# DeltaNet scan: the q-k matrices stored as full 128x128 blocks, one product a step, and buffers regrouped

## The chip, the cores and the metric

The kernel runs on one core of one Trainium2 chip. The core has a matrix engine (TensorE, PE in the rows, with PEld for the loading of its stationary operand), a vector engine (VectorE, DVE), a scalar engine (ScalarE, ACT), GpSimd (POOL), and SyncE (SP), which issues most DMAs. Each engine runs its own list of instructions in order, and waits for the others by semaphores. The metric is the device time of one execution in microseconds; less is better. All numbers are from the profiler's record of one execution, or from timed runs where this is said.

## The reference

One encoder layer over 768 tokens (a prompt of 256 and a sample of 512) with 1024 columns: a modulated norm, one input projection, eight heads of windowed attention beside four heads of a gated DeltaNet that runs forward and backward, an output projection, a second modulated norm and a gated feed-forward part. The change is in the DeltaNet. Its tokens are cut into chunks of 64, and each head and direction goes through its chunks with a state `S`:

```
a_mat = lower + jnp.eye(CHUNK)                      # lower = strict(kb k^T * decay)
u = triangular_solve(a_mat, v * beta)
w = triangular_solve(a_mat, kb * exp(gc))
intra = where(causal, (q k^T) * decay, 0)           # the q-k matrix of a chunk

def step(S, xs):
    v_new = u_i - w_i S
    o = q_i S + intra_i v_new
    S = S * exp(gl_i) + k_i^T v_new
```

## The kernel before

The program is written as ordinary code; a scheduler lays its instructions out for each engine by priority, and a pool hands out buffers by tag: a new tile under a tag with `bufs=1` can be written only when the last reader of the tile before it under that tag is done. So a tag that two tiles share is a wait, and a change of tags can change the order on every engine.

The heads of the DeltaNet are worked off in two pairs, called 0 and 1 here. For each pair:

- `dn_proj` makes q, k and v with the projection products L476. [...] The same line, with `z_proj`, and later `att_proj` (L868) serve as filler: they depend on little, and the scheduler puts them between the products of the scans and the solves.
- `dn_decay` (L616 to L629) makes the decay matrices: products L620, four `affine_select` on POOL, one exponential on ACT (L629).
- `dn_gram` (L634 to L651) multiplies them with k k^T and q k^T. The products L642 and L643 use 64 columns of the array each. The q-k matrices go into `Ic`, with 64 columns for each chunk.
- `dn_solve` inverts the triangular matrices. DVE does blocks of 16 by substitution (L691 and L693, 15 rounds, after the transpose L680 and the two L687, and before the transposes L695 and L700 and the two L701 and L702); PE joins them in levels (L708, L729). The result is `Wbd`.
- `dn_scan` (L752 to L806) goes through 24 steps: prompt and sample, two heads each, of four and eight steps. A step works on a forward and a backward chunk at once. On PE it has two products L768 (`S` against k and q), one L782 (`Wbd` times `r`), two L793 (the state's update) and two L802 (`Ic` times the new values). Between them DVE makes `r` (L774), half of `XS` (L786), the new `S` (L796) and the output (L806); ACT makes `tm` (L781), the other half of `XS` (L788) and the two copies `XB` (L790) of 64x128 each.

The two products of L802 take 64 columns of `Ic` each and write the two halves of the rows of one PSUM block `ps4`. Each takes a copy `XB` whose other half of rows is zero, which POOL has cleared once (L462), so that the forward chunk doesn't mix with the backward one:

```
for e in range(2):                                           # L789
    nc.scalar.copy(xb[half(e), e, :], ps2[half(e)])
...
for e in range(2):                                           # L801
    nc.tensor.matmul(ps4[half(1 - e)], Ic[:, j, tp, x, :], xb[:, e, :], start=True, stop=True)
```

After scan 1 come the attention (its q, k, v by L868, core from L939 on with buffers `sc`), the output projection (L1086), the second norm and the feed-forward part (L1169 and L1250). The order in which the program calls these parts is the order of their priorities: pair 0, pair 1's projections, scan 0, solve 1, `z_proj`, scan 1, attention.

Of the kernel before, what the change touches and what calls it, by code (L numbers as in the profile page):

```python
# [17 lines left out]
P = 128  # L18
T = 768
D = 1024  # L20
# [25 lines left out]
NV1 = VEC["n1g"][0]  # L46
NC1 = CST["bo"][0]
# [55 lines left out]
def layer(ctx: ExitStack, tc: tile.TileContext, I: dict, yout: bass.AP, dbg=None):  # L103
# [7 lines left out]
    vec = cpool.tile([P, VEC["_n"][1] - NV1], F32, name="vec")  # L111
# [3 lines left out]
    nc.sync.dma_start(vec[:], I["vec"][:, NV1:])  # L115
    nc.scalar.dma_start(cst[:], I["cst"][:, NC2:])

    vec2 = []

    def V(n, i=0, m=None):  # L120
        o, w = VEC[n]
        t_, o = (vec, o - NV1) if o >= NV1 else (vec2[0], o)
        return t_[:, o + i:o + (i + m if m is not None else w)]
# [14 lines left out]
    def load_w(pool, src, bufs, hp=HPW):  # L138
        """[128, 1024] weights -> (hi, lo)"""
# [11 lines left out]
    def rsqrt(out, v, shape, tag):  # L151
        """out = v ** -0.5 (v > 0), Newton on the integer seed"""
        a = small.tile(shape, F32, name="rs_a", tag="rs_a" + tag, bufs=2)
        ti = small.tile(shape, I32, name="rs_t", tag="rs_t" + tag, bufs=2)
# [23 lines left out]
    bw = cpool.tile([P, KD, 32], F32R, name="bw")  # L178
    braw = arow[:, 0:128].rearrange("p (k c) -> p k c", k=KD)
    nc.scalar.dma_start(braw, I["wba"])  # L180
    split(braw, bw[:, :, 0:16], bw[:, :, 16:32])

# [4 lines left out]
    def ada_piece(s, i, row, brow, load, PS, w4=None):  # L187
        """rows k = 4 i.. of set s; the four partial sums in rows 32 k.."""
# [26 lines left out]
    def ada_ahead(sets, row, bias, load, PS):  # L215
        """each piece is loaded a step before it is used"""
# [24 lines left out]
    # ================= mixer =================  # L241
    with ExitStack() as mx:
# [20 lines left out]
        with tc.tile_pool(name="st", bufs=1, reuse_waits="tile") as st:  # L263
# [13 lines left out]
            # x, features on partitions  # L277
# [7 lines left out]
            # rstd of the tokens, along the free axis  # L285
# [50 lines left out]
            # the first four products run along with the rows of h  # L336
# [32 lines left out]
        at = px.enter_context(tc.tile_pool(name="at", bufs=1, side="right", reuse_waits="tile"))  # L369
# [14 lines left out]
        def gates_dn():  # L384
# [13 lines left out]
            ba = dn.tile([P, NT, 16], F32, name="ba")  # L398
# [3 lines left out]
            def to_slots(dst, src):  # L402
                """src [P, t, (d h)] -> dst [P, h, t', d]"""
# [10 lines left out]
            beta = dn.tile([P, 4, NT, 2], F32, name="beta")  # L414
            to_slots(beta, e1[:])
            y1 = dn.tile(sc8, F32, name="y1")
            nc.vector.tensor_tensor(y1[:], ba[:, :, 8:16], V("dtb").unsqueeze(1).broadcast_to(sc8), ALU.add)
            y2 = dn.tile(sc8, F32, name="y2")
# [4 lines left out]
            na = dn.tile([P, 8], F32, name="na")  # L423
            nc.scalar.activation(na[:], V("alog"), AF.Exp)
            nc.vector.scalar_tensor_tensor(y1[:], y1[:], -1.0, na[:].unsqueeze(1).broadcast_to(sc8), ALU.mult, ALU.mult)
            gg = dn.tile([P, 4, NT, 2], F32, name="gg")
# [16 lines left out]
            pdec = dn.tile(s48, F32, name="pdec")  # L443
# [40 lines left out]
        def ada_bufs():  # L484
            """buffers that the heads have left: five for weights, one for the bias row"""
# [3 lines left out]
            for tag, shape in (("dec", [P, 24, 64]), ("MO", [P, 12, P])):  # L489
                a_ = dn.tile(shape, F32, name="au", tag=tag)[:].rearrange("p a b -> p (a b)")  # L490
                raws.append(a_[:, 0:1024].rearrange("p (k c) -> p k c", k=2))
# [4 lines left out]
        def ada_load(src):  # L496
            """four k of a set"""
# [85 lines left out]
        def dn_scales(hp, sqs):  # L583
            # sums of squares: natural for k, swapped halves for q
# [6 lines left out]
            rkk = dn.tile([P, 2, NT], F32, name="rkk", tag="rkk", bufs=2)  # L591
# [782 lines left out]
```

## Time and profile before

| what | value |
|---|---|
| median of 3 timed runs | 1194.71 us (1194.56 to 1194.93) |
| span of the profiled execution, first to last instruction | 1191.6 us |
| its mean granted TensorE clock, as a share of full speed | 0.981 |
| PE busy | 1150.3 us, 97% |
| DVE, ACT, POOL busy | 726.8, 539.0 and 69.0 us |
| scan 0 | 196.1 to about 274 us |
| substitution and levels of solve 1 | about 274 to 326.2 us |
| scan 1 | 326.2 to 407.6 us |
| attention, output projection, second norm | 407.6 to 640 us |
| feed-forward part | 640 to 1191.6 us |

The difference between the median and the span, 3.1 us, lies outside of the first and last instruction. The profile lists busy time by stretch (one line for each, with the clock that PE was granted), what an engine waited for, the chain of work that ended last in order of time, and single instructions on a timeline. Line numbers are those of the kernel before.

### The profile page before, as it was taken

The numbers are of one execution on the slowest core, as the hardware profiler recorded it, in microseconds if no ns is written. First come the engines' busy times: TensorE is split into PE (matmuls) and PEld (weight loads), VectorE is DVE, ScalarE is ACT, GpSimd is POOL, SyncE is SP. The second block draws the span as 40 slices with busy tenths as digits, with TensorE's granted clock in tenths as the row PEclk, the third lists the DMA queues.
The fourth block names the chain that finished last, engine by engine and source line by source line (L and its number), as shares of the span: only waits on it lengthen the run. The fifth ranks groups of instructions, "written<-read, shape, count | busy, mean of one in ns | idle before, by whom it ended". The sixth has DMA issues, their size and how long they took to land.

```text
span 1191.6 us, 17540 instructions
## 1 busy us (share of the span) xinstructions
PE 1150.3 (97%) x6682; PEld 940.3 (79%) x6682; DVE 726.8 (61%) x1544; ACT 539.0 (45%) x1301; POOL 69.0 (6%) x112
## 2 busy tenths in 40 slices
PE   6999899998999999999889999999999999999998
PEld 3778767777978698867678888888888888888886
DVE  5636986878476545364597655555655555564556
ACT  4357664574658666563476421430341233043310
POOL 1102103001100100100031000000000000000000
PEclk8999999999899999989999999999999999999999
DMA  8421142124241562281123411320311231031002
GB/s 306 197 71 36 54 142 90 58 94 142 73 149 55 176 231 72 76 264 60 59 75 106 142 54 29 113 66 6 115 63 36 71 89 53 18 102 58 19 1 106
DMA packets 43891, 110.98 MB, mean 93 GB/s; under 512 B 4384, under 2 KB 14528, under 8 KB 42528
## 3 DMA queue, kind: packets, MB, share of 16 engines
q1 hardware_dynamic: 36640, 92.93, 24.1%
q0 software_dynamic: 2928, 10.50, 2.7%
q10 hardware_dynamic: 4240, 6.44, 1.5%
q8 instruction: 52, 0.85, 0.3%
q14 instruction: 31, 0.25, 0.1%
HBM read 100.41 MB, written 9.45 MB: 92 GB/s over the span
## 4 chain that ended last, share of the span: by engine, by line
PE 79%; DVE 9%; ACT 7%; DMA 2%; issue 2%; SPq 0%; POOL 0%; DVEq 0%; ACTq 0%
PE dpt L1250 14%; PE upp L1169 10%; PE pjt L476 5%; PE pjt L868 4%; PE pat L1086 3%; PE sht L192 2%; PE pjt L345 2%; PE sdt L768 2%; ACT jk L884 1%; PE sdt L345 1%; PE sdt L944 1%; PE sdt L793 1%; PE sdt L802 1%; PE sdt L708 1%; PE mxt L970 1%
## 5 line engine op out<-in xcount | busy, mean ns | idle before, releaser
L136 DVE TENSOR_TENSOR wlo<-wraw,whi 128x1024 fp32r<-128x1024 f32 x72 | 88.1, 1223 | 115.9 <-ACT whi L135 115.7
L135 ACT CAST whi<-wraw 128x1024 fp32r<-128x1024 f32 x72 | 75.5, 1048 | 149.6 <-PE upp L1169 112.3
L1250 PE MATMUL dpt<-dh,gh 128*128 128x512 f32 x264 | 104.1, 395 | 0.2 <-DVE arow L1252 0.2
L1250 PE MATMUL dpt<-dl,gh 128*128 128x512 f32 x264 | 102.8, 389 | 0.0
L1250 PE MATMUL dpt<-dh,gl 128*128 128x512 f32 x264 | 102.3, 390 | 0.0
L1169 PE MATMUL upp<-h2lo,whi 128*128 128x256 f32 x352 | 99.8, 283 | 0.0
L1169 PE MATMUL upp<-h2hi,whi 128*128 128x256 f32 x352 | 98.8, 281 | 0.0
L1169 PE MATMUL upp<-h2hi,wlo 128*128 128x256 f32 x352 | 98.2, 279 | 0.0
L135 ACT CAST dh<-draw 128x1024 fp32r<-128x1024 f32 x22 | 23.1, 1052 | 160.4 <-PE dpt L1250 111.7
L1252 DVE TENSOR_TENSOR arow<-dpt,gb 128x512 f32<-128x512 f32 x72 | 49.8, 691 | 61.7 <-PE dpt L1250 59.6
L868 PE MATMUL pjt<-whi,hhi 128*128 128x256 f32 x288 | 85.4, 296 | 0.0
L868 PE MATMUL pjt<-whi,hlo 128*128 128x256 f32 x288 | 84.7, 294 | 0.0
L868 PE MATMUL pjt<-wlo,hhi 128*128 128x256 f32 x288 | 84.2, 292 | 0.0
L476 PE MATMUL pjt<-hhi,whi 128*128 128x512 f32 (+1 forms) x192 | 67.6, 352 | 1.3 <-DVE u L531 1.3
L476 PE MATMUL pjt<-hhi,wlo 128*128 128x512 f32 (+1 forms) x192 | 67.5, 353 | 0.0
L476 PE MATMUL pjt<-hlo,whi 128*128 128x512 f32 (+1 forms) x192 | 67.5, 352 | 0.0
L1169 PEld LDWEIGHTS upp<-h2hi,wlo 128*128 128x128 f32 x352 | 66.8, 190 | 0.2
L1169 PEld LDWEIGHTS upp<-h2hi,whi 128*128 128x128 f32 x352 | 66.3, 188 | 0.4
L1169 PEld LDWEIGHTS upp<-h2lo,whi 128*128 128x128 f32 x352 | 66.5, 189 | 0.0
L1250 PEld LDWEIGHTS dpt<-dh,gh 128*128 128x128 f32 x264 | 49.6, 188 | 13.4 <-DVE arow L1252 3.6
L868 PEld LDWEIGHTS pjt<-whi,hhi 128*128 128x128 f32 x288 | 55.9, 194 | 4.4 <-issue 3.6
L868 PEld LDWEIGHTS pjt<-whi,hlo 128*128 128x128 f32 x288 | 56.0, 195 | 2.5 <-issue 2.5
(910 smaller groups left out, 2882.7 us busy)
## 6 DMA issues: line engine op xcount, KB each, us to landing
wraw<-wup SPq DMA_DIRECT2D x44, 512.0 KB, 3.6
draw<-wdown SPq DMA_DIRECT2D x22, 512.0 KB, 3.5
araw<-ada SPq DMA_DIRECT2D x8, 1024.0 KB, 11.8
wraw<-wdn SPq DMA_DIRECT2D x16, 512.0 KB, 3.6
ew<-ada_w SPq DMA_DIRECT2D x16, 512.0 KB, 4.5
wraw<-wat SPq DMA_DIRECT2D x12, 512.0 KB, 4.1
sc<-abias POOLq DMA_DIRECT2D x24, 256.0 KB, 3.0
aw<-ada_w SPq DMA_DIRECT2D x10, 512.0 KB, 5.3
```

The lines of the kernel that those rows point to most:

```text
L135: nc.scalar.copy(hi, src)
L136: nc.vector.tensor_tensor(lo, src, hi.bitcast(F32), ALU.subtract)
L192: nc.tensor.matmul(p_[32 * kk:32 * kk + 32, :], cs[:, 4 * i + kk, :], w4[kk], start=True, stop=True)
L345: nc.tensor.matmul(o_, w0[i][w][:, k * P:(k + 1) * P], m[:, k, c0:c1], start=(k == 0 and n == 0 and (c0 > 0 or i % 2 == 0)), stop=(k == KD ...
L476: nc.tensor.matmul(o_, w[:, k * P:(k + 1) * P], m[:, k, c0:c1], start=(k == 0 and n == 0), stop=(k == KD - 1 and n == 2))
L708: nc.tensor.matmul(ps[:, n * 32:n * 32 + 32], M16[:, n, :], R[:, n, :], start=True, stop=True)
L768: nc.tensor.matmul(ps1[:, d * P:(d + 1) * P], KQ[:, j, tl[d], 2 * pr[d]:2 * pr[d] + 2, :].rearrange("p b c -> p (b c)"), St[:, d, :], star ...
L868: nc.tensor.matmul(o_, a[:, k, t * P:(t + 1) * P], w[kh][m][:, kk * 256:(kk + 1) * 256], start=(k == 0 and n == 0 and t % 2 == 0), stop=(k ...
L1086: nc.tensor.matmul(pt[:], m[:, a, j, :], w[:, sl], start=(j == 0 and n == 0), stop=(j == len(ks) - 1 and n == 2))
L1169: nc.tensor.matmul(o_, (lo if n == 2 else hi)[:, k * P:(k + 1) * P], (h2lo if n == 1 else h2hi)[:, k, c0:c1], start=(k == 0 and n == 0), s ...
L1250: nc.tensor.matmul(ps[:], a[:, t * P:(t + 1) * P], m[:, sl], start=(i == 0 and n == 0), stop=(i == len(gs) - 1 and n == 2))
L1252: nc.vector.tensor_tensor(arow[:], ps[:], gb[:, grp(t), sl], ALU.mult)
```

## The change

1. **The scan's q-k matrices.** `Ic` gets 128 columns for each chunk, its block in one half of the columns and zeros in the other; POOL clears all of it once for each pair (128x3072 elements). With the zeros in `Ic`, the copy needs none: one ACT copy of 128x128 goes into the step's own `r`, and one product of 128x128x128 replaces two. `XB` is gone. `r` has four buffers instead of two.
2. **Buffers.** The pool `at` is gone. The attention's raw q and k lie in the second half of the first `sc` tile (tag `Ic`, now 3072 elements), which is therefore allocated before the attention's projections. `rd` of `dn_decay` is under tag `MO`, and so waits for the solve before it; `bw` (the weights of beta and alpha) under tag `XS`, so that the clearing of `XS` waits for the products that read it; small tiles move as the diff shows. The output norm of the second scan has `so` and `fo` under tags `ssk` and `rkk`, and the norm of the queries `s_` and `f_` under `beta` and `pdec`. Some raw weights of the output projection and of the gates alternate between two places. 176 columns of the vector constants are loaded later, by POOL.

```
-            Ic = dn.tile([P, 2, NT, 2, 64], F32, name="Ic", tag="Ic", bufs=2)
+            Ic = dn.tile([P, 2, NT, 2, P], F32, name="Ic", tag="Ic", bufs=2)
+            nc.gpsimd.memset(Ic[:].rearrange("p h t x c -> p (h t x c)"), 0.0)
...
-                            nc.vector.tensor_tensor(Ic[r_, j, b:b + n, e if d == 0 else 1 - e, :],
+                            nc.vector.tensor_tensor(Ic[r_, j, b:b + n, e if d == 0 else 1 - e, (1 - e) * 64:(1 - e) * 64 + 64],
...
-                r = dn.tile([P, P], F32, name="r", tag="r", bufs=2)
+                r = dn.tile([P, P], F32, name="r", tag="r", bufs=4)
-                xb = XB[:, j]
...
-                for e in range(2):
-                    nc.scalar.copy(xb[half(e), e, :], ps2[half(e)])
+                nc.scalar.copy(r[:], ps2)
...
-                for e in range(2):
-                    nc.tensor.matmul(ps4[half(1 - e)], Ic[:, j, tp, x, :], xb[:, e, :], start=True, stop=True)
+                nc.tensor.matmul(ps4, Ic[:, j, tp, x, :], r[:], start=True, stop=True)
...
-            rd = at.tile([P, 24, 64], F32, name="rd", tag="raw")
+            rd = dn.tile([P, 24, 64], F32, name="rd", tag="MO")
...
-        XB = dn.tile([P, 2, 2, P], F32, name="XB", tag="XB")
-        nc.gpsimd.memset(XB[:], 0.0)
+        bw = dn.tile([P, KD, 32], F32R, name="bw", tag="XS")
+        split(braw, bw[:, :, 0:16], bw[:, :, 16:32])
...
-            so = dn.tile([P, 12], F32, name="so", tag="so")
-            fo = dn.tile([P, 12], F32, name="fo", tag="fo")
+            so = dn.tile([P, 12], F32, name="so", tag="ssk", bufs=2)
+            fo = dn.tile([P, 12], F32, name="fo", tag="rkk")
...
-            raw = at.tile([P, NT, 4, 64], F32, name="raw", tag="raw", bufs=1)
+            raw = rest[0].rearrange("p (t h c) -> p t h c", t=NT, h=4)
-            s_ = at.tile([P, 24], F32, name="s_", tag="s_")
-            f_ = at.tile([P, 24], F32, name="f_", tag="f_")
+            s_ = dn.tile([P, 24], F32, name="s_", tag="beta")
+            f_ = dn.tile([P, 24], F32, name="f_", tag="pdec")
...
-                raw = wo.tile([P, D], F32, name="wraw", tag="wraw", bufs=WRB)[:]
+                raw = wo.tile([P, D], F32, name="wraw", tag="wraw")[:] if i % 2 else rest[1][:, 0:D]
...
-                    raw = wo.tile([P, KD, P], F32, name="mraw", tag="wraw", bufs=WRB)
+                    raw = (wo, wm)[t % 2].tile([P, KD, P], F32, name="mraw", tag="wraw")
...
+        vec3.append(fp.tile([P, VEC["_n"][1] - NV2], F32, name="vec3"))
+        nc.gpsimd.dma_start(vec3[0][:], I["vec"][:, NV2:])
```

**What it moves.** The order of the instructions on each engine changes in three places. The first is ACT in solve 0. `dec` is the exponential of the decay (L629 before, L628 after), `KQ` the silu of pair 1's projections, `whi` a cast of weights. Before:

```order
L555 COPY Vt<-sht 128x256
L555 COPY Vt<-sht 128x512
L629 ACTIVATE dec<-dec 128x1536
L529 ACTIVATE u<-pjt,vec_616 128x256
L135 CAST whi<-wraw 128x1024
L548 ACT_TABLE_LOAD
L548 ACTIVATE KQ<-u 128x6x2x64
```

and after:

```order
L554 COPY Vt<-sht 128x512
L136 CAST whi<-wraw 128x1024
L528 ACTIVATE u<-pjt,vec_610 128x256
L547 ACT_TABLE_LOAD
L547 ACTIVATE KQ<-u 128x6x2x64
L528 ACTIVATE u<-pjt,vec_610 128x512
L628 ACT_TABLE_LOAD
L628 ACTIVATE dec<-dec 128x1536
L528 ACTIVATE u<-pjt,vec_610 128x256
```

The exponential stands behind a weight cast, two evacuations of pair 1's projections and a silu, and the tables of the functions are loaded once more on either side of it (L628 here, and again for the silu L545 behind it). On DVE, in the same place, the product that needs it (L634 before, L635 after; `Vt` are the values scaled by `vs`) stood behind two scalings:

```order
L595 TENSOR_TENSOR vs<-vs,ssk 128x12
L610 TENSOR_SCALAR Vt<-Vt,vs 128x128 x2
L634 TENSOR_TENSOR dec<-dec,pp 128x1536
L530 SCALAR_TENSOR_TENSOR u<-pjt,vec_616,u 128x255
L136 TENSOR_TENSOR wlo<-wraw,whi 128x1024
```

and now stands behind all twelve of the pair and two more evacuations:

```order
L594 TENSOR_TENSOR vs<-vs,ssk 128x12
L609 TENSOR_SCALAR Vt<-Vt,vs 128x128
L137 TENSOR_TENSOR wlo<-wraw,whi 128x1024
L529 SCALAR_TENSOR_TENSOR u<-pjt,vec_610,u 128x255
L609 TENSOR_SCALAR Vt<-Vt,vs 128x128
L530 SCALAR_TENSOR_TENSOR u<-pjt,vec_610,u 128x255
L609 TENSOR_SCALAR Vt<-Vt,vs 128x128 x10
L529 SCALAR_TENSOR_TENSOR u<-pjt,vec_610,u 128x511
L530 SCALAR_TENSOR_TENSOR u<-pjt,vec_610,u 128x511
L635 TENSOR_TENSOR dec<-dec,pp 128x1536
```

The second place is DVE at the end of scan 0, where the substitution of solve 1 begins (L680 to L693 before, L681 to L694 after). Before, its first instructions stand between those of the scan's last steps:

```order
L680 STREAM_TRANSPOSE Wbd<-sv 128x1024
L796 SCALAR_TENSOR_TENSOR S_1262<-S_1262,egl,sdt 128x128 x2
L786 TENSOR_TENSOR XS<-sdt,pex 64x128
L806 TENSOR_TENSOR Wbd<-sdt,tm 128x128
L774 SCALAR_TENSOR_TENSOR r<-sdt,negc,Vt 64x128 x2
L796 SCALAR_TENSOR_TENSOR S_1263<-S_1263,egl,sdt 128x128 x2
L786 TENSOR_TENSOR XS<-sdt,pex 64x128
L687 SCALAR_TENSOR_TENSOR sv<-Wbd,cst_618,sv 128x16x16
L806 TENSOR_TENSOR Wbd<-sdt,tm 128x128
L774 SCALAR_TENSOR_TENSOR r<-sdt,negc,Vt 64x128 x2
L687 SCALAR_TENSOR_TENSOR sv<-Wbd,cst_618,sv 128x16x16
L691 TENSOR_TENSOR Wbd<-sv 128x2
```

and after:

```order
L210 SCALAR_TENSOR_TENSOR A_77<-sht,vec 128x8
L681 STREAM_TRANSPOSE Wbd<-sv 128x1024
L805 TENSOR_TENSOR Wbd<-sdt,tm 128x128
L775 SCALAR_TENSOR_TENSOR r<-sdt,negc,Vt 64x128 x2
L805 TENSOR_TENSOR Wbd<-sdt,tm 128x128
L817 TENSOR_TENSOR Vt<-Wbd 64x512 x2
L688 SCALAR_TENSOR_TENSOR sv<-Wbd,cst_612,sv 128x16x16 x2
L805 TENSOR_TENSOR Wbd<-sdt,tm 128x128
L692 TENSOR_TENSOR Wbd<-sv 128x2
L817 TENSOR_TENSOR Vt<-Wbd 64x512 x2
L694 TENSOR_REDUCE sv<-Wbd 128x2
```

The transpose stands where the scan has only its last two outputs and one `r` left, and the rounds (`Wbd<-sv`) begin behind the scan's last output L805. The third place is PE in scan 0. Before, a step's two half products (`64x128`) stand between full ones:

```order
L768 MATMUL sdt<-S_1263,KQ 128x128
L476 MATMUL pjt<-hhi,wlo 128x512
L802 MATMUL sdt<-XB,Ic 64x128 x2
L782 MATMUL sdt<-r,Wbd 128x128
L768 MATMUL sdt<-S_1263,KQ 128x128
```

and after, one full product stands in such a place:

```order
L793 MATMUL sdt<-XS,Kt 128x128 x2
L769 MATMUL sdt<-S,KQ 128x128
L801 MATMUL sdt<-r,Ic 128x128
L769 MATMUL sdt<-S,KQ 128x128
L475 MATMUL pjt<-hlo,whi 128x256
L475 MATMUL pjt<-hhi,wlo 128x256
```

Counted over whole stretches, PE's order also changes in how many filler products stand ahead of a point:

| products ahead of | L476, 512 columns | L476, 256 columns | L192, 512 columns | L868, 256 columns |
|---|---|---|---|---|
| first L708 of solve 0, before / after | 192 / 204 | 169 / 192 | 12 / 16 | 0 / 0 |
| first product of scan 0 (L782) | 202 / 216 | 192 / 213 | 16 / 20 | 0 / 0 |
| last product of scan 0 (L802, L801) | 278 / 288 | 264 / 279 | 32 / 32 | 0 / 0 |
| first L708 of solve 1 | 288 / 288 | 288 / 288 | 32 / 32 | 71 / 132 |
| first product of scan 1 (L782) | 288 / 288 | 288 / 288 | 32 / 32 | 169 / 212 |
| last product of scan 1 | 288 / 288 | 288 / 288 | 56 / 56 | 369 / 403 |

On POOL the eight copies of values into `r` (L777) of each scan now stand together, ahead of the four copies into `MO` (L678) in scan 0 and ahead of the first three loads of `sc` in scan 1. On SP the load for the output projection's fifth block moves ahead of loads of the residual `X2`, two loads of `wup` move ahead of one of the gates' weights (`mraw`), and another `mraw` load now waits for the release of the mixer's memory.

## Rows read from the trace of the kernel before

**Rows 1.** page, first line: the span

```profile
span 1191.6 us, 17540 instructions
```

**Rows 2.** stretches: window us, busy PE PEld DVE ACT POOL, PE clock

```profile
196.10:274.10 78.00, 77.36 (x538) 56.45 (x539) 60.19 (x179) 51.53 (x141) 10.32 (x17) 1.00 0.22 72
274.10:294.60 20.50, 17.18 (x122) 15.62 (x123) 19.95 (x45) 9.46 (x32) 2.82 (x5) 0.99 0.60 205
...
326.20:407.60 81.40, 80.16 (x581) 59.04 (x580) 55.06 (x162) 52.79 (x184) 1.16 (x4) 1.00 0.32 105
```

**Rows 3.** what PE waited for, 270 to 327 us: total, times, longest us

```profile
PE sdt L708 <- DVE Wbd L701: 3.3, 1, 3.3
```

**Rows 4.** chain that ended last, 196 to 408 us: shares by line

```profile
by line: PE pjt L476 10.2%; PE pjt L868 10.0%; PE sdt L768 8.5%; PE sht L192 7.4%; PE sdt L793 7.0%; PE sdt L802 6.6%; PE sdt L782 5.8%; PE sdt L708 3.7%; ACT tm L781 3.2%; ACT XB L790 2.9%; ACT jk L884 2.8%; PE sdt L729 2.8%; DMA zz<-zd 2.
```

**Rows 5.** chain in scan 0: start us, us to the next piece, what

```profile
222.12 0.37 PE sdt L802 x4
222.48 0.42 PE sdt L782 x2
...
228.44 0.22 PE sdt L782 x2
```

**Rows 6.** chain in scan 0, later

```profile
254.31 0.64 PE sdt L768 x4
...
260.79 0.45 PE sdt L793 x4
```

**Rows 7.** timeline of PE in scan 0: start us, us of the group, instruction

```profile
229.06 0.44 PE L802 MATMUL sdt<-XB,Ic 128*64 128x128 f32 x4
...
229.76 0.39 PE L476 MATMUL pjt<-hhi,whi 128*128 128x512 f32 x1
230.00 0.40 PE L476 MATMUL pjt<-hlo,whi 128*128 128x512 f32 x1
```

**Rows 8.** timeline of PEld there, idle before in brackets

```profile
229.06 0.20 PEld L802 LDWEIGHTS sdt<-XB,Ic 128*64 128x64 f32 x4 [0.25 <-DVE S L796]
```

**Rows 9.** chain where halves stand among halves

```profile
209.63 0.22 PE sdt L802 x4
209.85 0.21 PE sht L643 x2
```

**Rows 10.** ACT copies, 196 to 408 us, by form: busy us, mean ns | idle before

```profile
L790 ACT COPY XB<-sdt 64x128 f32<-64x128 f32 x96 | 24.9, 259 | 7.1 <-PE sdt L782 5.0 <-PE sdt L802 0.6
...
L804 ACT COPY Wbd<-sdt 128x128 f32<-128x128 f32 x8 | 2.1, 262 | 1.3 <-PE sdt L802 1.2
```

**Rows 11.** timeline of ACT in solve 0

```profile
118.66 1.49 ACT L629 ACTIVATE dec<-dec 128x1536 f32<-128x1536 f32 x1
...
125.72 1.28 ACT L548 ACT_TABLE_LOAD   x1 [4.27 <-DVE u L531]
127.01 0.85 ACT L548 ACTIVATE KQ<-u 128x768 f32<-128x768 f32 x1
```

**Rows 12.** timeline of DVE: solve 0's L634, solve 1's L680

```profile
121.92 1.75 DVE L634 TENSOR_TENSOR dec<-dec,pp 128x1536 f32<-128x1536 f32 x1
...
259.64 2.02 DVE L680 STREAM_TRANSPOSE Wbd<-sv 128x1024 f32<-128x1024 f32 x1
...
293.61 0.87 DVE L701 SCALAR_TENSOR_TENSOR Wbd<-sv,cst,Wbd 128x384 f32<-128x384 f32 x1
```

**Rows 13.** chain in solve 1

```profile
294.62 5.30 PE sdt L708 x24
...
305.13 2.61 PE sdt L708 x24
...
317.59 5.52 DMA zz<-zd
...
324.61 1.54 PE pjt L868 x13
```

**Rows 14.** busy time and PE clock behind that wait

```profile
294.60:300.00 5.40, 5.38 (x25) 5.40 (x26) 0.67 (x1) 1.54 (x4) 0.00 (x0) 0.50 0.01 3
```

More of the change, by code (lines that the diff above doesn't have):

```diff
@@ L46 @@
 NV1 = VEC["n1g"][0]
+NV2 = VEC["fcw"][0]
 NC1 = CST["bo"][0]
@@ L151, in rsqrt @@
     def rsqrt(out, v, shape, tag):
-        a = small.tile(shape, F32, name="rs_a", tag="rs_a" + tag, bufs=2)
-        ti = small.tile(shape, I32, name="rs_t", tag="rs_t" + tag, bufs=2)
+        a = small.tile(shape, F32, name="rs_a", tag="rs_a" + tag, bufs=2 if tag == "1" else 1)
+        ti = small.tile(shape, I32, name="rs_t", tag="rs_t" + tag, bufs=2 if tag == "1" else 1)
         nc.vector.tensor_scalar(ti[:], v.bitcast(I32), 1, None, ALU.logical_shift_right)
@@ L488, in ada_bufs @@
             raws.extend(w_[:, i] for i in range(3))
-            for tag, shape in (("dec", [P, 24, 64]), ("MO", [P, 12, P])):
-                a_ = dn.tile(shape, F32, name="au", tag=tag)[:].rearrange("p a b -> p (a b)")
+            for tag in ("dec", "MO"):
+                a_ = dn.tile([P, 1536], F32, name="au", tag=tag)
                 raws.append(a_[:, 0:1024].rearrange("p (k c) -> p k c", k=2))
@@ L747, in dn_scan @@
         def dn_scan(hp, KQ, Kt, Vt, pex, Ic, Wbd):
-            S = [[dn.tile([P, 2, P], F32, name=f"S{s}{j}", tag=f"S{s}{j}") for j in range(2)] for s in range(2)]
+            S_ = dn.tile([P, 4, 2, P], F32, name="S", tag="S")
+            S = [[S_[:, 2 * s + j] for j in range(2)] for s in range(2)]
             half = lambda e: slice(e * 64, e * 64 + 64)
@@ L874, in att_qk @@
         def att_qk(hf, which, QT):
-            raw = at.tile([P, NT, 4, 64], F32, name="raw", tag="raw", bufs=1)
+            raw = rest[0].rearrange("p (t h c) -> p t h c", t=NT, h=4)
             def ev(ps, t):
-                nc.scalar.copy(raw[:, t:t + 2].rearrange("p t h c -> p (t h c)"), ps[:])
+                nc.scalar.copy(rest[0][:, t * 256:t * 256 + 512], ps[:])
             att_proj(hf * 3 + which, ev)
-            s_ = at.tile([P, 24], F32, name="s_", tag="s_")
-            f_ = at.tile([P, 24], F32, name="f_", tag="f_")
+            s_ = dn.tile([P, 24], F32, name="s_", tag="beta")
+            f_ = dn.tile([P, 24], F32, name="f_", tag="pdec")
             for i in range(24):
-                jk = at.tile([P, 64], F32, name="jk", tag="jka", bufs=1)
+                jk = dn.tile([P, 64], F32, name="jka")
                 nc.scalar.activation(jk[:], raw[:, i // 4, i % 4, :], AF.Square, accum_out=s_[:, i:i + 1])
@@ L886, in att_qk @@
             rsqrt(f_[:], s_[:], [P, 24], "24")
-            r3 = raw[:].rearrange("p t h c -> p (t h) c")
+            r3 = rest[0].rearrange("p (n c) -> p n c", c=64)
             nc.vector.tensor_tensor(r3, r3, f_[:].unsqueeze(2).broadcast_to([P, 24, 64]), ALU.mult)
@@ L1018, in layer @@
         QT = []
+        scs, rest = [], []
+        for i in range(2):
+            sc3 = dn.tile([P, 6, 512], F32, name="sc", tag="Ic", bufs=2)
+            scs.extend(sc3[:, u] for u in range(3))
+            rest.append(sc3[:, 3:6].rearrange("p a b -> p (a b)"))
         def take(g, n):
@@ L1031, in layer @@
         att_half(0, iter(()), (0, 0, 0))
-        pTs = [dn.tile([P, 512], F32, name="pT", tag=t)[:] for t in ("XS", "XB")]
-        scs = []
-        for _ in range(2):
-            sc3 = dn.tile([P, 3, 512], F32, name="sc", tag="Ic", bufs=2)
-            scs.extend(sc3[:, u] for u in range(3))
+        pTs = [dn.tile([P, 512], F32, name="pT", tag=t)[:] for t in ("XS", "S")]
         core = att_core(0, QT[0], SD, SD, [(a, b, u) for a in range(2) for b in range(2) for u in range(3)])
```

36 lines of the change are left out of this document (16 added, 20 removed).

## The prediction

> **What bounds the kernel now.** I read the busy time by stretch first. The profiled execution lasts 1191.6 us [rows 1]; 3.1 us lie outside of it up to the median of 1194.71, and I take them as unchanged. The change touches the two scans and the solves around them. In scan 0 PE is busy for 77.36 of 78.0 us, in scan 1 for 80.16 of 81.4, both at the full granted clock; DVE and ACT stand at 50 to 60 us there [rows 2]. So both scans are bound by the sum of PE's work: the dependencies of a step are hidden behind filler products. Between them lies the opposite case. From 274.1 to 294.6 DVE is busy for 19.95 of 20.5 us with the substitution of solve 1, and PE waits 3.3 us for it at the end [rows 2, 3]. So what is saved on PE in scan 0 is given back there, unless the filler that it makes room for comes off later. The list of what PE waited for was the second view, the chain of work the third: in it L802 has 6.6% of the 212 us from 196 to 408, 14.0 us, and L790 (the copies) 2.9%, 6.1 us [rows 4].
>
> **The scan's step on PE.** A full product of 128x128x128 takes 0.22 us to the start of the next piece ("x2", since each is two passes) [rows 5]. The two half products (x4) take 0.37, and the product behind them then takes 0.42 instead of 0.22 [rows 5]; where two products stand behind them, 0.64 instead of 0.45 [rows 6]. So a pair of halves among full products costs 0.37 + 0.20 = 0.57 us. The timeline shows where it goes: the weights for the halves are not loaded ahead as others are, they start at 229.06, together with their product, after 0.25 us in which the loader stood idle [rows 7, 8]. The change puts one full product in its place: 0.57 - 0.22 = **0.35 us a step**, 24 steps a scan, 8.4 us a scan, **16.8 us in all**. The bounds: only those on the chain count, 14.0 / 0.37 = 38 groups, 38 x 0.35 = 13.3 us; or nothing at all, if the price comes from the place and not from the form. For that end there is one kind of row: where halves stand among other halves (L643), the four take 0.22 and the next halves 0.21, no more than their number [rows 9]. Nearly all of the steps stand among full products, as rows 5 and 6 do, so I take 16.8.
>
> [...]
>
> **The copies on ACT.** Two copies of 64x128 took 0.26 us each, and one of 128x128 takes 0.26 as well [rows 10]. That is 48 x 0.26 = 12.5 us off ACT, half of 6.1 us off the chain. Since PE's sum is the bound there, I count 0 and keep 3 us for the range. The wider `Ic` costs DVE nothing: the same number of elements is written.
>
> **Solve 0, where the order gets worse.** Before, the exponential ended at 118.66 + 1.49 = 120.15 and L634 at 121.92 + 1.75 = 123.67 [rows 11, 12]. Now it stands behind pair 1's first silu. That silu ended at 127.86 [rows 11]; its input waited on DVE behind L634, which no longer stands in front (1.75 us), so 126.1. Then come an evacuation (no longer than the silu's 0.85), a table load of 1.28, the exponential 1.49 and L634 1.75: 131.4, **7.7 us later** than before. All of solve 0 hangs on it. What hides it is filler: 12 projections of 512 columns, 23 of 256 and 4 L192 more stand ahead of its first L708 on PE. One of 512 takes 0.24 from start to start [rows 7], 13 of 256 took 1.54, so 0.12 each [rows 13]; I price L192 as 512 columns. That is 2.9 + 2.8 + 1.0 = 6.6 us. So PE waits **1.1 us** more. The bounds are 0 (the older waits hidden in this stretch go first) and 4 (the weight cast ahead of the exponential waits for its buffer).
>
> **Scan 0.** Ahead of its first L782 stand 14, 21 and 4 more of these, 6.8 us; with the 1.1 it starts 7.9 us later, at 204.0. Inside are 4, 6 and 4 fewer, 2.6 us, and the 8.4 are saved: it lasts 78.0 - 11.0 = 67.0 and ends at 271.0, **3.1 us earlier** than before [rows 2].
>
> **Substitution of solve 1.** Before, L680 started at 259.64 [rows 12] and the first rounds ran between the scan's last steps. Now L680 stands just ahead of the scan's last outputs, and the rounds behind them. DVE's 20.5 us from the scan's end to the L708 stay, and the work that was done before it comes on top: two L687, and nine small instructions of the first rounds. I set it at 3 us, from L680's 2.02 for 1024 columns (the L687 have 256 each) and a few tenths for each small one; the bounds are 2 and 5. So the first L708 starts at 271.0 + 20.5 + 3 = 294.5, against 294.62: **scan 0's gain ends here**. It isn't lost, though: 132 products L868 stand ahead of this point instead of 71, 61 x 0.12 = 7.3 us of the attention's projections that come off later.
>
> **Levels of solve 1.** The chain from the first L708 to the first product of scan 1 takes 31.5 us and goes through a wait of 5.52 us for a DMA [rows 13], none of which gets shorter. PE has 80 products L868 to put in there instead of 98: it waits 18 x 0.12 = **2.1 us** longer. Scan 1 starts at 326.1, as before.
>
> **Scan 1 and the rest.** It saves its 8.4 us, and has 191 fillers L868 instead of 200, 1.1 us: it ends 9.5 us earlier. Behind it 34 fewer L868 remain, 4.0 us, and after them the order on PE is nearly the same. So the end comes 9.5 + 4.0 = **13.5 us earlier**; or, from the other side, 16.8 saved less 1.1 and 2.1 of new waiting. 1194.7 - 13.5 = **1181.2 us**. Clearing `Ic` on POOL and the later loads I count at nothing: POOL is busy 10 us in 78 [rows 2]. If a load of `mraw` or `wup` waits for the mixer's memory, one load, about the 5.5 us of the DMA in rows 13, could come on top; or as much less, since two `wup` loads move ahead.
>
> **The rivals.**
> - *Less is left of scan 0 (1186 to 1191.5).* If the lateness of solve 0 isn't covered and the substitution has the upper bounds, 4 instead of 1.1 and 5 instead of 3, PE waits 5 us more: 1186; with a late load, 1191.5. For it: DVE has no slack in that stretch [rows 2].
> - *More (1171 to 1176).* If the substitution ends 3 us sooner, PE no longer stands idle ahead of L708. [...] Without the wait, up to 3.3 us and some 5 of the clock come back: 1173.
> - *The halves cost nothing (1192).* If a pair of halves is no dearer than one full product, only the copies' 3 us remain: 1191.7, and a new wait of 1.1 makes it 1192.8. Rows 5 and 6 speak against it, rows 9 for it. [...]
> - *Slower: the clock (1203).* The scans are covered by filler that now is used up sooner, 7 us of it before scan 0. If a step's chain shows through and PE pauses, the granted clock falls as it did behind the 3.3 us wait [rows 3, 14], and PE's work takes twice as long: 22 us of it, a third of scan 0, would cost 22 us, 1181.2 + 22 = 1203. It decides from 13.5 us of work at the lower level. Against it: both scans hold a clock of 1.00 [rows 2], and 138 projections of pair 1 are left inside scan 0.
> - *Shifted without gain (1192 to 1196).* Several small waits in the regrouped buffers eat the gain; no row names one.
>
> **How the numbers follow.** The forecast, 1176 to 1187 with 1181 as its time: 0.55. Less: 0.14. More: 0.13. Halves cost nothing: 0.06. Slower by the clock: 0.07. No gain: 0.05. A measurement of this kernel can tell 0.2%, 2.4 us, from no change. Faster by more: the first three and a third of the fourth, 0.84. Slower by more: the clock and a fifth of the last, 0.08. The rest, 0.08, is the same. The range of 8 in 10 is 1173 to 1191.5: it leaves out the last three cases and the end of "more".
>
> **What would show it.** Right: no half products in the scan, the product behind L801 back at 0.22, scan 1 shorter by 8 to 10 us with PE still above 97% busy; L634 some 8 us later; scan 0 starting later and ending near 271, the first L708 of solve 1 still near 294, and the gain visible only behind scan 1. Wrong in size: the first L708 of solve 1 at 290 or 300, or a stretch in the scans with a clock under 1. Wrong in kind: full products at 0.35 or more behind one another in the scan, or the time from 408 to the end longer than before.

## The result, and the profile after

The changed kernel takes **1187.63 us** (median of four runs, 1186.39 to 1191.23), the kernel before on the same chip 1194.68. The ratio is **0.9943, interval 0.9927 to 0.9959**: about 7 us faster. The forecast was 13.5 us, 1181. The sign was right and the time lies inside the range of 8 in 10 (1173 to 1191.5), but just outside 1176 to 1187, the range with the largest chance: the size was off by half, so the question is where the other half went.

The stretches of the changed kernel, which answer to [rows 2]. Columns: window, its length, then busy us (instructions) of PE, PEld, DVE, ACT, POOL, the clock that PE was granted, the DMA share and GB/s:

```profile
201.30:277.00 75.70, 74.58 (x491) 57.74 (x489) 59.07 (x161) 46.32 (x122) 12.37 (x19) 1.00 0.22 68
277.00:298.00 21.00, 17.10 (x143) 16.89 (x142) 20.29 (x52) 11.10 (x36) 2.15 (x5) 0.97 0.57 197
298.00:320.00 22.00, 21.19 (x147) 21.02 (x148) 9.13 (x16) 12.41 (x47) 2.80 (x3) 0.80 0.08 25
320.00:400.90 80.90, 79.74 (x570) 63.50 (x569) 57.44 (x168) 51.14 (x185) 0.00 (x0) 1.00 0.41 132
400.90:510.00 109.10, 102.01 (x727) 88.19 (x725) 48.38 (x159) 68.58 (x232) 10.21 (x19) 0.98 0.44 144
```

Both scans are as full as before (PE above 98% at a clock of 1.00), and DVE is full in the substitution behind scan 0. The stretch behind scan 1 has the new hole: PE idles for 7.1 of 109.1 us there. Before, it idled for 2.2 us in the 102.4 us behind scan 1:

```profile
407.60:510.00 102.40, 100.18 (x739) 87.33 (x738) 43.45 (x146) 63.87 (x227) 10.24 (x19) 1.00 0.44 146
```

The marks of the two profiled executions, in us from the start of each:

| point | before | forecast | after |
|---|---|---|---|
| decay product of solve 0 (L634, L635) | 121.9 | +7.7 | 128.5 (+6.6) |
| first product of scan 0 | 196.1 | 204.0 | 201.3 |
| last product of scan 0 | 277.1 | 271.0 | 276.9 |
| first level product of solve 1 (L708, L709) | 294.6 | 294.5 | 298.1 |
| first product of scan 1 | 326.0 | 326.1 | 325.3 |
| last product of scan 1 | 407.3 | 9.5 earlier | 400.6 (6.7 earlier) |
| end | 1191.6 | 13.5 earlier | 1185.9 (5.7 earlier) |

Nothing of the change's effect is visible at the end of scan 0. All of it comes out behind solve 1, as forecast, and it is half as large.

**Where it went.** The span splits into three parts: time in which PE stood idle, time that PE lost at the lower clock (half of its busy time in stretches where the granted clock is 0.50; projections of 256 columns come every 0.21 us there instead of every 0.12), and the rest, PE's work as it would be at the full clock:

| kernel | span | PE idle | lost at the lower clock | PE's work |
|---|---|---|---|---|
| before | 1191.6 | 41.3 | 18.2 | 1132.0 |
| after | 1185.9 | 45.8 | 20.0 | 1120.1 |

The work fell by 11.9 us (16.8 forecast), the idle time rose by 4.5 (3.2 forecast), and the clock took 1.8 more (0 forecast). So some five of the eight us of the gap lie in the one term that carried the forecast, PE's work.

**Why a full product isn't 0.22 us here.** Three places on PE's timeline of the changed kernel. Columns: start us, us of the group, instruction; "x2" are the two passes of one product (96 records for 48 products):

```profile
213.75 0.27 PE L643 MATMUL sht<-KQ 128*64 128x128 f32 x1
213.95 0.49 PE L801 MATMUL sdt<-r,Ic 128*128 128x128 f32 x2
214.37 0.32 PE L644 MATMUL sht<-KQ 128*64 128x128 f32 x1
...
236.59 0.40 PE L475 MATMUL pjt<-hhi,whi 128*128 128x512 f32 x1
236.88 0.49 PE L801 MATMUL sdt<-r,Ic 128*128 128x128 f32 x2
237.12 0.48 PE L475 MATMUL pjt<-hlo,whi 128*128 128x512 f32 x1
237.44 0.38 PE L801 MATMUL sdt<-r,Ic 128*128 128x128 f32 x2
...
268.64 0.38 PE L769 MATMUL sdt<-S,KQ 128*128 128x128 f32 x2
268.86 0.39 PE L801 MATMUL sdt<-r,Ic 128*128 128x128 f32 x2
269.08 0.39 PE L769 MATMUL sdt<-S,KQ 128*128 128x128 f32 x2
```

Among the scan's own products (268.86) it takes 0.22 to the next start. Between two projections (236.88) it takes 0.24, it starts 0.29 behind a projection that otherwise takes 0.24, and the projection behind it takes 0.32: 0.37 in all. Between products of 64 columns (213.95) it takes 0.42. Over both scans, worked out from the starts of all such groups: the distance from a group's start to the next start, plus what the instruction ahead and the one behind take above their usual 0.24 (512 columns), 0.12 (256) or 0.11 (one pass of a scan product). Rarer combinations are left out, and so is what a product into `sht` loses that stands next to the group. The places are 46 after since some products stand together; before, a step whose passes are strewn among L642 and L643 counts as several. The products into `sht`, by the lines of the kernel before, are narrow ones (L642, L643 with 64 columns of the array, L192 with 32, L199 with 2) and full ones (L620, L894):

| neighbours, in order | one full product, after | two half products, before |
|---|---|---|
| scan, then scan | 0.23 (7 places) | 0.57 (8) |
| projection, then projection | 0.32 (17) | 0.61 (12) |
| projection, then scan | 0.37 (7) | 0.62 (8) |
| product into `sht`, then scan | 0.29 (9) | 0.48 (7) |
| such on both sides | 0.35 (3) | 0.27 (7) |
| mean of all steps | **0.306** | **0.524** |

The gain is 0.52 - 0.31 = 0.22 us a step, 10.5 us for 48 steps, not 0.35 and 16.8. The busy column would never have shown it. The group's own rows, by form, from 190 to 410 us, of before and then of after (busy us, mean ns | idle ahead of it):

```profile
L802 PE MATMUL sdt<-XB,Ic 128*64 128x128 f32 x192 | 20.8, 296 | 0.1
```

```profile
L801 PE MATMUL sdt<-r,Ic 128*128 128x128 f32 x96 | 19.9, 292 | 0.1
```

By these, the change saves 0.9 us. Busy times of products overlap: the projection at 236.59 has 0.40 us, and the next product starts 0.29 us behind it. By the distances to the next start, with the time lost at the lower clock taken off, the group's own rows fall by 5.7 us, and the other 6.2 of the 11.9 stand in rows of other products.

**The new wait.** What PE waited for from 100 to 430 us in the changed kernel (total, times, longest):

```profile
PE sdt L709 <- DVE Wbd L702: 5.2, 2, 4.0
PE sdt L841 <- ACT Vt L836: 3.0, 1, 3.0
```

The longest of the first is the old wait of [rows 3], 4.0 instead of 3.3. The second is new, in the output norm behind scan 1. ACT there (start us, us, instruction, idle ahead in brackets), and PE:

```profile
412.63 0.98 ACT L836 ACTIVATE Vt<-Vt,fo 128x128 f32<-128x128 f32 x3
417.76 0.34 ACTq L846 DMA_DIRECT2D mixn<-zz  x1
418.15 0.40 ACT L836 ACTIVATE Vt<-Vt,fo 128x128 f32<-128x128 f32 x1 [4.54 <-DMA Vp<-vd]
...
418.61 0.33 PE L841 MATMUL sdt<-cst,Vt 128*128 128x128 f32 x1 [3.00 <-ACT Vt L836]
...
419.49 0.28 PE L867 MATMUL pjt<-whi,hlo 128*128 128x256 f32 x1
419.61 0.38 PE L867 MATMUL pjt<-wlo,hhi 128*128 128x256 f32 x1
419.79 0.41 PE L867 MATMUL pjt<-whi,hhi 128*128 128x256 f32 x1
420.00 0.41 PE L867 MATMUL pjt<-whi,hlo 128*128 128x256 f32 x1
```

The twelfth scaling (L836) is queued on ACT behind the first store of the mixer's output (L846), the store is issued 4 us late, with a load of other data (`Vp<-vd`) as the last event before it, and PE's products queue behind it. When PE goes on, the projections soon come every 0.21 instead of 0.12 us: the granted clock is 0.50 for 3.4 us, from 419.65 to 423.06.

### The profile page after: what moved, and what is told of

The parts are those of the page before. It is cut to its first block, busy times and chain, and to the rows that moved or that the text cites. A ratio compares the mean times of both kernels' runs of the same rounds, so it can differ in the third digit from the quotient of the medians.

```text
span 1185.9 us, 17290 instructions
## 1 busy us (share of the span) xinstructions
PE 1140.1 (96%) x6586; PEld 941.7 (79%) x6586; DVE 726.7 (61%) x1544; ACT 527.5 (44%) x1255; POOL 70.1 (6%) x114
## 4 chain that ended last, share of the span: by engine, by line
PE 51%; DVE 4%; ACT 1%; issue 1%; POOL 0%; DVEq 0%; ACTq 0%
PE dpt L1252 14%; PE upp L1171 10%; PE pat L1086 3%; PE mxt L968 1%; DVE arow L1254 1%; DVE X L1255 1%; PE sdt L943 1%; PE sht L961 1%; PE ups__6308 L1171 1%; PE ups__8714 L1171 0%; PE ups__8858 L1171 0%; PE ups__8851 L1171 0%; PE ups__8721 L1171 0%; PE ups__8584 L1171 0%; PE ups__8577 L1171 0%
## 5 line engine op out<-in xcount | busy, mean ns | idle before, releaser
L136 ACT CAST dh<-draw 128x1024 fp32r<-128x1024 f32 x22 | 23.1, 1050 | 158.2 <-PE dpt L1252 111.7
L867 PEld LDWEIGHTS pjt<-wlo,hhi 128*128 128x128 f32 x288 | 56.5, 196 | 2.5 <-issue 2.5
```

What stands on the lines that cost most here:

```text
L136: nc.scalar.copy(hi, src)
L867: nc.tensor.matmul(o_, a[:, k, t * P:(t + 1) * P], w[kh][m][:, kk * 256:(kk + 1) * 256], start=(k == 0 and n == 0 and t % 2 == 0), stop=(k ...
```

## The experiments

All of them are edits of the changed kernel. In the diffs, "-" is the changed kernel, and the lines around are left out. Ratios are to the kernel before, run on the same chip.

### The product alone: both scans, scan 0, scan 1

Undone is only the product: two half products of `Ic` again, with the one copy and all buffers as changed.

```
-                nc.tensor.matmul(ps4, Ic[:, j, tp, x, :], r[:], start=True, stop=True)
+                for m in range(2):
+                    nc.tensor.matmul(ps4[half(m)], Ic[:, j, tp, x, m * 64:m * 64 + 64], r[:], start=True, stop=True)
```

> The changed kernel, with the one product of a scan step made again as two half products (64 columns of Ic each, same r, same single copy on ACT). Theory A (the forecast's size): a pair of halves costs 0.35 us more than a full product and the saving reaches the end: 48 x 0.35 = 16.8 us, 1187.6 + 16.8 = 1204. Theory B (from the trace of the changed kernel): a full product has a price of its own among the projections, the difference is 0.58 - 0.32 = 0.26 us a step, 12.6 us, 1200. Rival: halves cost nothing and the gain came from the buffers and the order: 1188.

Measured: 1196.19 us, ratio 1.0010 (0.9998 to 1.0022). The whole gain is gone, 8.6 us above the changed kernel; the two sizes that were expected, 16.8 and 12.6, were both too large. PE's work is 1129.3 us, 9.2 above it. The old wait at the end of solve 1's substitution is longer, too:

```profile
PE sdt L709 <- DVE Wbd L702: 6.4, 1, 6.4
```

Then the same only where `hp == 0` (scan 0), and only where `hp == 1` (scan 1):

> The changed kernel, with two half products in scan 0 only. If scan 0's saving reaches the end in full, by the filler that comes off later: 6.3 us (24 x 0.26), 1194. If it is given back in the substitution of solve 1, where DVE is the bound: 0 to 2 us, 1188 to 1190.

> The changed kernel, with two half products in scan 1 only. Nothing DVE-bound stands behind scan 1, so all of it should reach the end: 24 x 0.26 = 6.3 us, 1194. If the saving of scan 1 is lost in the new wait behind it (PE waits 3.0 us for ACT's L836 at 415 us), it would come back as less: 1188 to 1190, since a later scan would find the loads done.

Measured: halves in scan 0 alone 1193.90 us, 0.9992 (0.9974 to 1.0010); in scan 1 alone 1191.79 us, 0.9976 (0.9961 to 0.9992). Undoing scan 0 costs 6 us, undoing scan 1 costs 4, and PE's work is 4.8 and 5.5 us above the changed kernel's. So **both scans' savings reach the end**, with the one copy of the changed kernel. What scan 0 saves is not visible at the first L709, because filler runs there instead, and it comes back later as filler that is already done. That part of the forecast held.

### The price is the change of form

The halves made twice (two pairs behind each other, same target), and the full product made twice:

```
-                nc.tensor.matmul(ps4, Ic[:, j, tp, x, :], r[:], start=True, stop=True)
+                for m in range(2):
+                    nc.tensor.matmul(ps4[half(m)], Ic[:, j, tp, x, m * 64:m * 64 + 64], r[:], start=True, stop=True)
+                for m in range(2):
+                    nc.tensor.matmul(ps4[half(m)], Ic[:, j, tp, x, m * 64:m * 64 + 64], r[:], start=True, stop=True)
```

```
                 nc.tensor.matmul(ps4, Ic[:, j, tp, x, :], r[:], start=True, stop=True)
+                nc.tensor.matmul(ps4, Ic[:, j, tp, x, :], r[:], start=True, stop=True)
```

> As e1_halves, with the pair of half products of each step made twice in a row (four half products into the same rows; the second pair repeats the first). Theory: a pair of halves is dear for the change from full to half columns and back, 0.1 us on each side and 0.15 more than a full product inside; a second pair behind the first needs no change and costs its own 0.22 us: PE's work grows by 48 x 0.22 = 10.6 us against e1_halves, 1196 + 10 = 1206. Rival: each pair of halves has its price of 0.37 by itself, wherever it stands: 48 x 0.37 = 17.8 us, 1214.

> The changed kernel, with the full product of each step made twice in a row. The second one stands behind a product of its own kind and costs 0.22 us: 48 x 0.22 = 10.6 us of PE's work, 1187.6 + 10 = 1198, if both scans are bound by PE's sum. If PE had slack in the scans (its waits there hide work), less: 1190 to 1194.

Measured: 1201.39 us (ratio 1.0047, 1.0029 to 1.0064) and 1197.81 us (1.0026, 1.0008 to 1.0044). The second full products cost the 10 us that were expected; the second pairs cost some 5, where 10 were expected and 18 by the rival. PE's timeline with the pairs made twice, L802 the first pair and L804 the second:

```profile
226.24 0.39 PE L804 MATMUL sdt<-r,Ic 128*64 128x128 f32 x4
226.46 0.38 PE L644 MATMUL sht<-KQ 128*64 128x128 f32 x2
...
227.47 0.39 PE L769 MATMUL sdt<-S,KQ 128*128 128x128 f32 x2
227.79 0.44 PE L802 MATMUL sdt<-r,Ic 128*64 128x128 f32 x4
228.06 0.39 PE L804 MATMUL sdt<-r,Ic 128*64 128x128 f32 x4
228.37 0.49 PE L783 MATMUL sdt<-r,Wbd 128*128 128x128 f32 x2
228.70 0.39 PE L769 MATMUL sdt<-S,KQ 128*128 128x128 f32 x2
```

L769 takes 0.32 in front of a pair instead of 0.22, the first pair 0.27, the second 0.31, and L783 behind it 0.33 instead of 0.22. Where a product of the same 64 columns follows (226.24), a second pair takes 0.22, so I read 0.10 of the 0.31 as the way back. Against 0.22 for a full product, changing to 64 columns and back costs some 0.36 us, and a second pair in the same form 0.21, no more than a full product. Over the kernel, by the distances to the next start, the second pairs add 9.3 us to the rows of the first ones (0.19 each), and the second full products 11.7 (0.24 each); other products gain some of it back, and PE's work grows by 6.3 and 10.3. So two half products are dear for the change, not for their number. These rows give about 0.1 us ahead of the pair, 0.05 in it, and 0.2 behind it.

In both scans and the solves around them (100 to 430 us) PE changes its column form 149 times before and 76 times after. What remains are mostly the products of 64 and 32 columns (L643, L644, L191) strewn in as filler. It is beside these and beside projections that the full product is dearer than 0.22 (0.29 to 0.37 on average).

### The wait behind scan 1

The second scan's stores of the mixer's output go to POOL's queue instead of ACT's:

```
-                nc.scalar.dma_start(mixn[2 + hp][j], z)
+                (nc.gpsimd if hp else nc.scalar).dma_start(mixn[2 + hp][j], z)
```

> The changed kernel, with the two stores of the second scan's output (mixn from zz) issued by POOL instead of ACT, so that ACT's last L836 no longer stands behind a store that waits for the loads of Vp. Theory: PE's wait of 3.0 us at 415 goes, and with it the stretch of 3.4 us at half clock behind it (1.7 us): 1187.6 - 4.7 = 1183, and no new low clock near 420. Rival: the time goes into the next wait (the attention's loads), 1187 to 1188.

Measured: 1188.47 us, ratio 0.9942 (0.9927 to 0.9957), no difference to the changed kernel. What PE waited for from 100 to 460 us:

```profile
PE sdt L709 <- DVE Wbd L702: 6.0, 2, 4.8
PE sht L893 <- DVE sc L887: 2.9, 1, 2.9
```

The wait on L841 is gone, so the store on ACT's queue was its cause; but one of nearly the same length stands in the attention (L893). The granted clock from 420 to 460 us averages 0.96 in both kernels, so about as much time at half clock is left there. So taking this one wait away gains nothing. That the filler which used to cover both is used up by then would explain it, but was only argued.

### The copies, and the old step in the new buffers

Two copies of 64x128 instead of one, first with the full product, then with the two half products (the old step in all but `XB`):

```
-                nc.scalar.copy(r[:], ps2)
+                for e in range(2):
+                    nc.scalar.copy(r[half(e)], ps2[half(e)])
```

> The changed kernel, with the copy into r made as two copies of 64x128 on ACT, as before the change. ACT gets 48 x 0.26 = 12.5 us more in the scans. The forecast: hidden, 0 to 3 us, 1188 to 1191. Rival: ACT's chain shows through in a step, 24 steps of the two samples' chains at 0.26: 6 us, 1194.

> The changed kernel with both parts of the scan's step as before: two copies of 64x128 and two half products (of the full-width Ic). What is left of the change is the regrouped buffers and the order. Theory: these cost time by themselves, by the later solve 0 and new waits on PE (1 us before the scans, 3 us behind scan 1): against the kernel before +1 to +5 us, 1196 to 1200. Rival: the regrouping is worth something by itself (earlier loads): 1190 to 1194.

Measured: with the full product 1190.16 us, 0.9957 (0.9941 to 0.9973), 2.5 us over the changed kernel's first measurement: the copies are nearly hidden, as counted. With the halves, **1188.72 us, 0.9943 (0.9928 to 0.9958): as fast as the whole change**. Both expectations, 1196 to 1200 and 1190 to 1194, were above that. It contradicts the first experiment, unless the one copy more or less changes what the product is worth.

### The four together

So the four combinations ran again, one after the other on one chip:

> The changed kernel again, on one chip with the three that follow: one copy, one full product. Question of the four: is the distance between the pair of half products with one copy (1.0010 of the kernel before) and with two copies (0.9943) a property of the programs, or of the chips and executions on which each was seen? If of the programs (their order of instructions): 0.994 again here, the wait of 3.0 us on the state's copy behind the second scan again, and half clock at the same places (about 297, 420, 508 and 587 us). If of the executions: the ratio moves by 0.003 or more, or the half-clock stretches of more than 3.4 us lie elsewhere.

> The changed kernel with two half products and one copy. If the order of the program sets it: 1.001 again, 8 us above the changed kernel, the wait in front of the second substitution 6 to 6.5 us again. If the executions set it: it comes nearer to the old step with two copies, 0.995 to 0.998.

> The changed kernel with one full product and two copies. If the product gives its 8 to 10 us whatever stands around it: 8 us under the old step with two copies. If the order takes it back here: within 3 us of the old step with two copies, as on the other chip, at about 0.9955.

> The changed kernel with two half products and two copies, the old step in the new buffers. If the order of the program sets it: 0.994 again, level with the changed kernel, with half-clock time 5 us less in sum than the changed kernel's. If the executions set it: 0.998 to 1.002, level with two halves and one copy, and its half-clock time about that of the others.

| | one full product | two half products |
|---|---|---|
| one copy | 1188.06 us, 0.9941 (0.9923 to 0.9959) | 1197.37 us, 1.0018 (1.0009 to 1.0028) |
| two copies | 1190.62 us, 0.9973 (0.9960 to 0.9986) | 1190.33 us, 0.9971 (0.9951 to 0.9990) |

The pattern stands, so it belongs to the programs. With one copy the product is worth 9 us of time. With two copies it is worth nothing that can be measured: the second measurement gives 0.3 us against it, the first 1.4. The parts of the spans, for the profiled execution of each of the two measurements (as the table above):

| kernel | span | PE idle | lost at the lower clock | PE's work |
|---|---|---|---|---|
| full, one copy (the change) | 1185.9, 1184.5 | 45.8, 47.2 | 20.0, 15.6 | 1120.1, 1121.7 |
| halves, one copy | 1193.9, 1192.1 | 47.1, 45.2 | 17.5, 17.2 | 1129.3, 1129.7 |
| full, two copies | 1188.0, 1187.2 | 44.7, 45.1 | 17.6, 16.9 | 1125.8, 1125.2 |
| halves, two copies | 1188.5, 1191.6 | 44.0, 42.4 | 13.9, 19.0 | 1130.6, 1130.1 |

- *Work.* It repeats to within 2 us. The product saves 9.2 and 8.0 with one copy, but only 4.8 and 4.9 with two. Its own rows save nearly the same in both (5.8 and 5.4); what differs is what other products lose beside their neighbours. With the full product, the second copy changes the order on PE so that other groups take longer, in both measurements alike: 2.0 us more for the 32-column products of L191, 1.4 and 1.3 for the projections of `whi` by `hlo`, 1.0 for the two products of `S`.
- *Waits.* With halves, the second copy takes the wait at the end of solve 1's substitution from 6.4 and 5.6 us down to 3.5 in both measurements. Halves with one copy and with two, second measurement, 185 to 330 us:

```profile
PE sdt L709 <- DVE Wbd L702: 5.6, 1, 5.6
```

```profile
PE sdt L709 <- DVE Wbd L702: 3.5, 1, 3.5
```

- *Clock.* One profiled execution misleads here: the one of halves with one copy in the second measurement was the fastest of ten timed runs, the one of halves with two copies the slowest of seven. But each timed run has its granted clock on record. Medians of the timed runs, first and second measurement (and, for the kernel before, its runs beside the three groups of experiments); the last column is (1 - clock) x span, an upper bound of the time lost, since it also counts the time at the lower clock in which PE idled:

| kernel | runs | span | granted clock | lost, at most |
|---|---|---|---|---|
| full, one copy (the change) | 4, 4 | 1185.5, 1186.0 | 0.982, 0.981 | 21.3, 23.1 |
| halves, one copy | 10, 10 | 1194.2, 1195.3 | 0.982, 0.980 | 21.5, 23.9 |
| full, two copies | 5, 10 | 1188.4, 1188.7 | 0.982, 0.983 | 21.4, 20.2 |
| halves, two copies | 4, 7 | 1186.8, 1188.4 | 0.987, 0.986 | 16.0, 16.7 |
| before | 25, 14, 22 | 1193.5, 1192.8, 1192.7 | 0.979, 0.980, 0.981 | 25.1, 23.9, 22.7 |

So halves with two copies, the old step in the new buffers, was granted a higher clock than all others, in both measurements, as was expected of it at the second. With the last column taken off, the product is worth 8 us with one copy (7.9 and 8.4) and still 3 to 4 with two (3.9 and 2.8); with two copies the clock takes that back. The same accounts for the kernel before, which by the spans is 4 to 6 us slower than its old step in the new buffers: with the last column taken off it is 1 to 2 us faster.

The two kernels with halves lie 3.0 us apart in their profiled executions on average (1193.0 and 1190.05), and 7 by their medians. Waiting accounts for the 3.0, and the granted clock is enough for the rest: the last column differs by 5.5 and 7.2 us, and among the kernel before's own timed runs one us of it goes with 0.6 to 0.7 us of span, so I estimate 3 to 5 us. What stays open is why one order of the same work is granted the higher clock. A kernel with the new product in the old buffers wasn't run either, so the share of the product and that of the buffers in the 7 us of the whole change aren't separated outside of the new buffers.

No kernel here beats the changed one by more than the measurement tells.

## Why the prediction was right or wrong

- **What bounds the kernel: right.** Both scans are still bound by the sum of PE's work, at a clock of 1.00; the full product made twice cost some 10 us, what it adds to PE's work there.
- **The scan's step on PE: this is the step that failed, as a size.** It priced the pair of halves at 0.57 and the full product at 0.22, from [rows 5, 6], and said that nearly all steps stand among full products. In fact 9 of the 48 steps before stood beside products of 64, 32 or 2 columns and 6 more beside other products into `sht`; there a pair costs 0.27 to 0.48 ([rows 9] was the sign of it, and was set aside). And only 7 of 46 full products after stand among the scan's own. The others stand beside projections or products into `sht`, at 0.29 to 0.37 on average. The term was 0.22 a step and 10.5 us by the neighbours' table (PE's work, undone alone: 9.2 and 8.0), not 0.35 and 16.8. The bound of 13.3 was no bound: it counted fewer steps, at the same price.
- **The copies: nearly right by time, wrong in kind.** Counted at 0, bound 3. A second copy costs 2.5 us with the full product, and saves 7 with the halves, by a shorter wait and a higher granted clock. That a copy would set the order of everything else was in no rival.
- **Solve 0: right.** L635 came 6.6 later (7.7 forecast); PE's idle time from 110 to 185 us rose from 3.7 to 4.7 (1.1 forecast). Scan 0 then began 5.2 us later, not 7.9: from 110 us to its first product PE's work grew by 5.7 us (6.8 forecast), and PE lost 1.7 us less at the lower clock.
- **Scan 0: wrong by twice.** It became 5.4 us shorter, not 11.0. The price above makes 3.1 of the missing 5.6; the rest was not traced. And its end before was misread: the last half products start at 276.9 to 277.1, not 274.1.

```profile
276.94 0.44 PE L802 MATMUL sdt<-XB,Ic 128*64 128x128 f32 x4
```

- **Substitution of solve 1: right in kind.** The first L709 stands where the scan's end and DVE put it. From the scan's last product to it are 21.2 us. The forecast had 23.5, but from the misread end; from the right one it was 17.5 before, so the added DVE time is 3.7 (3 forecast). The scan ended 5.9 later than forecast, so the first L709 came at 298.1 and not at 294.5. DVE, in the order of time:

```profile
277.26 0.28 DVE L805 TENSOR_TENSOR Wbd<-sdt,tm 128x128 f32<-128x128 f32 x1
277.46 0.15 DVE L692 TENSOR_TENSOR Wbd<-sv 128x2 f32<-128x2 f32 x1
...
293.81 1.92 DVE L696 STREAM_TRANSPOSE sv<-sv 128x1024 f32<-128x1024 f32 x1
```

- **Levels of solve 1: wrong.** The 31.5 us from the first L708 to scan 1 were taken as a chain that can't get shorter, with 2.1 us of new waiting for want of filler. They took 27.2 us, with 18 fewer fillers (2.2 us) and less waiting: from 285 to 330 us PE idled for 4.9 us instead of 5.5, and of that 0.9 instead of 2.2 behind the wait for the substitution. The DMA of 5.52 us in [rows 13] was on the chain that ended last, but PE had filler beside it, and waited only 0.9 us at its end before:

```profile
PE sdt L842 <- DVE zz L845: 0.9, 1, 0.9
```

  This made up most of what scan 0 lacked: scan 1 began at 325.3, 326.1 forecast.
- **Scan 1 and the rest: half right.** Scan 1 ended 6.7 us earlier (9.5 forecast). Behind it, 4.0 us of fillers fewer should have come off; instead the rest took 1.0 us longer, with 3.0 in the wait on L841 and 1.7 lost at half clock behind it.
- **The rivals.** "Less is left" gave 1186 to 1191.5 and holds the time, but by luck: the waits it named came out near the forecast (1.0 for 1.1, 3.7 for 3), far from its bounds of 4 and 5. "More" and "slower" didn't come: the wait ahead of L709 grew to 4.0, and both scans kept a clock of 1.00. Of the 1173 in "more", the 5 us of clock are half of the 9.8 us at 0.50 behind the wait of 3.3 us (294.6 to 304.4 before); no run shows that they come back without it, and behind the longer wait of the changed kernel there were 8.9 us at 0.50 (298.1 to 307.0). "Halves cost nothing" is refuted by the halves with one copy, 8.6 and 9.3 us dearer; with two copies its time, no gain from the product, was the result, though PE's work still fell by 4.8.

## What to carry to other kernels

Price a change of form on TensorE by the distance of starts, the neighbours' included, at all kinds of places where the instruction stands, weighted by how many there are; a single clean row gives the best case (0.22 us here, 0.31 on average). In a kernel whose filler covers nearly every wait, an edit's effect is the work it saves only as long as the scheduler's order stays: one ACT copy more made the same edit worth 9 us or none. So test an edit in two orders before its gain is called its own, and compare the granted clock of all timed runs before a difference is called work or waiting: one profiled execution can be the fastest or the slowest of its kernel, as here of ten and of seven.

## What the runs showed of the hardware

- In the rows at 227.47 to 228.70, a change from 128 to 64 columns and back cost some 0.36 us among full fp32 products of 0.22 us (0.1 ahead, 0.05 within, 0.2 behind; 0.10 of the last is an estimate from the row at 226.24), and a second pair in the narrow form 0.21.
- A lone 128x128x128 product between projections cost 0.32 us on average over 17 places instead of 0.22, though both use all 128 columns: there, too, the next instruction started later (0.32 instead of 0.24 behind the product at 236.88).
- A wait of 3.0 us on PE was followed by 3.4 us at the clock of 0.50 in one execution of the changed kernel (the rows at 419.61 to 420.00), whose granted clock was 0.981 over the span. Another execution, with 2.9 us at the same place, had 0.985, and PE lost 15.6 us instead of 20.0 at the lower clock:

```profile
PE sdt L841 <- ACT Vt L836: 3.2, 2, 2.9
```

- Programs with nearly the same work on PE (1129.3 and 1129.7 us, 1130.6 and 1130.1) were granted different clocks in most of their runs: halves with one copy 0.982 and 0.980, with two copies 0.987 and 0.986 (medians of 10, 10, 4 and 7 timed runs).
